# S5 powers, table and C moved to VectorE and ScalarE, and the first S5 chunk run through the K tiles together with one output-gate chunk

## The chip, the cores and the metric

The kernel runs on one core of one Trainium2 chip. The metric is the device time of one execution in microseconds (us); lower is better. The core's engines run side by side: TensorE (PE in the profile) multiplies matrices, and its weight loads (PEld) are listed apart; VectorE (DVE) and GpSimd (POOL) do element-wise work, ScalarE (ACT) does activations and copies, SyncE (SP) issues most transfers. Each engine carries out its own instructions in a fixed order.

## The reference

One layer of a streaming encoder over 272 positions (16 learned meta tokens and 256 inputs), width 2048, all in float32:

```
proj = rmsnorm(h) @ w_in                  # 2048 x 5120, columns q | f | i | g | u, 1024 each
o_hg = hgrn2(q, f, i) * norm * silu(g)    # gated linear recurrence, 8 heads of 128
y    = scan(x_t = A x_(t-1) + B u_t), C x # S5: 64 groups, 64 complex states each
o_s5 = rmsnorm(glu(gelu(y + d*u), w_glu)) # 1024 x 1024
h    = h + [o_hg, o_s5] @ w_out           # 2048 x 2048
h    = h + convffn(rmsnorm(h))            # w_gate, w_up, w_down with 5632 columns, width-3 convolution
out  = rmsnorm(h[16:])
```

S5 needs per state: the discretised A (`abr`, `xi`), its powers as cosines and sines of multiples of an angle, the factor (`zr`, `zi`) of B, and C.

## The kernel before, in words

**Weights.** Every weight matrix goes through in units of 1024 x 256 (1 MB): one DMA into a `raw` buffer (three of them), and then in two halves ACT rounds to `whi` and DVE takes the rest as `wlo` (L163 and L85, 128x1024 each; three buffers of each). A product is three matmuls, L187 (hi x hi), L188 (whi x low part of the input) and L189 (wlo x hi). The first two units (`early`) are split by DVE and POOL in quarters.

**Chunks.** A chunk of 256 columns of `w_in` is two units (K tiles 0 to 7 and 8 to 15) into two PSUM accumulators `acc` of 128 rows, 96 matmuls. There are 20 chunks: four each of u (S5), f, q, i (HGRN2; `do_h` runs one of each) and g (output gate). `ORDER` sets their order: u0 h0 u1 h1 u2 h2 u3 h3 g0 g1 g2 g3. The pool `pmm` has three accumulators; of the five other PSUM banks one, `psc`, serves the HGRN2 scores.

**Inputs.** xT is normalised K tile by K tile: `xn` on DVE, `xh` rounded on ACT, `xl` the rest on DVE (272 wide). The first chunk waits for these tiles one by one.

**S5 parameters.** About 60 instructions of 32 columns on DVE give `pw[0]` (cosine, sine of one step), abr, xi, zr, zi and the products zar, zai. POOL then makes eight more powers (`cpow`) and the table `ew` of 17 steps. C is loaded by SP, widened by two POOL copies, turned by 16 transposes, and DVE makes `cpc` from it in twelve instructions of 512 columns (two "kinds"). Scratch for this lies in two big tiles, `sca` and `scb`, which share their buffers (tags "gs" and "oT", one buffer each) with the tiles `gs` (gate times gain, all heads) and `oT` (HGRN2 output) that follow.

**Buffers.** A pool gives a buffer to the next tile of a tag only when every instruction that uses the earlier tile has run. In the pool `hgp` each tag has one buffer unless the line says otherwise; `sg` is the tag of the gate's sigmoid in `hg_g` and of q's in `hg_q`, and of `qt` in `hg_group`.

**Order on an engine.** The tool that builds the program orders each engine's instructions ahead of time: of those it takes for ready, the one of the highest priority. Priority is the order of the program text, shifted by `pri(...)`: weight splitting is moved up most (-4), reading accumulators by -3, `hg_group` by -2; the chunk's matmuls are moved down by 1.

The S5 scan of a group (`s5_scan`) and HGRN2's group work are mostly DVE work and run behind the chunks. After g3 the S5 part is finished: `gh` is made from the last S5 tile, then four w_glu chunks, then w_out.

Of the kernel before, what the change touches and what calls it, by code (L numbers as in the profile page):

```python
# [18 lines left out]
T = SEQ + NM  # L19
# [54 lines left out]
def hymba_kernel(ctx: ExitStack, tc: tile.TileContext, x, meta, lb_logits, norm_mix, w_in, hg_norm,  # L74
# [9 lines left out]
    def tt(dst, a, b, op, eng=dve):  # L84
        eng.tensor_tensor(out=dst, in0=a, in1=b, op=op)  # L85
# [82 lines left out]
    def colunit(w, k, c):  # L168
        return w[k * 1024:(k + 1) * 1024, c * 256:(c + 1) * 256].rearrange("(a p) n -> p a n", p=128)

    wpri = [1]

    def mm3(accs, units, rhs, n0, n1):

        last = len(units) - 1
        for ui, (u, k0) in enumerate(units):
            for hf, (hi, lo) in enumerate(u):
                for m in range(2):
                    for k in range(4):
# [39 lines left out]

    sca = ogp.tile([128, NH * NQ], F32, tag="gs", name="sca")  # L220
    scb = ogp.tile([128, NH * NQ], F32, tag="oT", name="scb")
    nrow = sca[0:KD, 256:384]

    xT = resp.tile([128, KD, T], F32, name="xT")
    hT = xT[:, :, T0:T]
# [1 line left out]
    sp.dma_start(out=ident, in_=c_ident)  # L227
    sp.dma_start(out=xm, in_=meta)
    HD = D // 2
    vrow = sca[0:100, 0:128]  # L230
    srow = sca[0:96, 128:256]
    lrow = prm.tile([96, 2], F32, name="lrow")
    crow = prm.tile([66, 2, 128], F32, name="crow")
    pool.dma_start(out=srow[0:32], in_=lam_re.rearrange("o (j g) p -> (o j) (g p)", g=2))
# [193 lines left out]
    tt(tz, zi, xi, MUL)
    tt(zar, zar, tz, SUB)
    tt(zai, zr, xi, MUL)  # L430
    tt(tz, zi, abr, MUL)
    tt(zai, zai, tz, ADD)
# [13 lines left out]
    tt(lbc[:, 0], le, le, SUB)  # L446
    ts(lbc[:, 1], lbc[:, 0], -1.0, MUL, 1.0, ADD)

    pt2 = prm.tile([128, 2, NP], F32, name="pt2")
    pt3 = prm.tile([128, 2, NP], F32, name="pt3")  # L450

    def cpow(dst, a, b):
        tt(pt2, pw[:, a, 1:3], pw[:, b, 1:2].to_broadcast([128, 2, NP]), MUL, pool)
        tt(pt3, pw[:, a, 0:2], pw[:, b, 2:3].to_broadcast([128, 2, NP]), MUL, pool)
        tt(pw[:, dst, 1:3], pt2, pt3, ADD, pool)
        ts(pw[:, dst, 0], pw[:, dst, 2], -1.0, MUL, 0.0, ADD, pool)

    for d_, a_, b_ in ((1, 0, 0), (2, 1, 1), (3, 2, 2), (4, 3, 3), (5, 4, 4), (6, 5, 1), (7, 6, 6), (8, 7, 7)):
        cpow(d_, a_, b_)
# [5 lines left out]
    et2 = scb[:, 1024:1536].rearrange("p (j s b) -> p j s b", j=NP, s=2)
    et3 = scb[:, 1536:2048].rearrange("p (j s b) -> p j s b", j=NP, s=2)
    for lv, n in ((1, 1), (2, 2), (3, 4), (4, 8)):
        cb = pw[:, lv, 1].unsqueeze(2).unsqueeze(3).to_broadcast([128, NP, 2, n])
        sb = pw[:, lv, 2].unsqueeze(2).unsqueeze(3).to_broadcast([128, NP, 2, n])
        tt(et2[:, :, :, 0:n], ew[:, :, 1:3, 0:n], cb, MUL, pool)  # L470
        tt(et3[:, :, :, 0:n], ew[:, :, 0:2, 0:n], sb, MUL, pool)
        tt(ew[:, :, 1:3, n:2 * n], et2[:, :, :, 0:n], et3[:, :, :, 0:n], ADD, pool)
        ts(ew[:, :, 0, n:2 * n], ew[:, :, 2, n:2 * n], -1.0, MUL, 0.0, ADD, pool)
    for k in range(3):
        dve.tensor_copy(out=ew[:, :, k, 16:17], in_=pw[:, 5, k].unsqueeze(2))


    cx = sca[:, 0:2048].rearrange("p (r b g q) -> p r b g q", r=2, b=8, g=2)
    craw = scb[:, 0:1024].rearrange("p (r b q) -> p r b q", r=2, b=8)
# [3 lines left out]
    cpc = s5p.tile([128, NP, 2, 2, S5H], F32, name="cpc")
    cq = [scb[:, 512 * i:512 * i + 512].rearrange("p (j h) -> p j h", h=S5H) for i in range(2)]
    ct = [sca[:, 512 * i:512 * i + 512].rearrange("p (j h) -> p j h", h=S5H) for i in range(2)]
    for ri in range(2):
        for hb in range(2):
            tp = ptp.tile([128, 4, 128], F32, tag="tp", name="ctp")
            with pri(LATE):
              for b in range(4):  # L490
                pe.transpose(tp[:, b], cx[:, ri, hb * 4 + b].rearrange("p a b -> p (a b)"), ident)
            for g in range(2):
                pr = slice(64 * g, 64 * g + 64)
                act.copy(out=cq[ri][pr, hb * 16:(hb + 1) * 16, :],
                         in_=tp[pr].rearrange("p b (j g h) -> p (b j) g h", g=2, h=S5H)[:, :, g])
    for kind, (wr, wi) in enumerate(((zr, zi), (zar, zai))):
        wrb = wr.unsqueeze(2).to_broadcast([128, NP, S5H])
        wib = wi.unsqueeze(2).to_broadcast([128, NP, S5H])
        tt(ct[0], cq[0], wrb, MUL)
        tt(ct[1], cq[1], wib, MUL)  # L500
        tt(cpc[:, :, kind, 0], ct[0], ct[1], SUB)
        tt(ct[0], cq[0], wib, MUL)
        tt(ct[1], cq[1], wrb, MUL)
        stt(cpc[:, :, kind, 1], ct[0], -1.0, ct[1], MUL, SUB)
# [67 lines left out]
    def s5_scan(P_, bu):  # L572

        W = s5w.tile([128, 3, TH], F32, tag="W", name="W", bufs=3)
        tmp = s5w.tile([128, 2, 68], F32, tag="tmp", name="tmp")
        act.copy(out=W[:, :, 0:17], in_=ew[:, P_])
        for lv, n in ((6, 17), (7, 34), (8, 68)):
            fact(tmp[:, :, 0:n], W[:, 0:2, 0:n], AF.Copy, scale=pw[:, lv, 2, P_:P_ + 1])
            stt(W[:, 1:3, n:2 * n], W[:, 1:3, 0:n], pw[:, lv, 1, P_:P_ + 1], tmp[:, :, 0:n], MUL, ADD)
# [197 lines left out]
        return accs  # L777


    def do_u(c):  # L780
        accs = chunk(w_in, 16 + c)
        with pri(-3):
            for m in range(2):
                s5_u(2 * c + m, accs[m])
        for m in range(2):
            s5_tile(2 * c + m, *s5_split(2 * c + m), *s5_b(2 * c + m))

    def do_h(g):
        accs = chunk(w_in, 4 + g)
# [270 lines left out]
```

## Time and profile before

| what | us |
|---|---|
| median of 3 runs (lowest, highest) | 1244.62 (1244.57, 1245.36) |
| the profiled execution's own time | 1245.69 |
| its span, first to last instruction | 1243.9 |
| PE busy in the span | 1219.3 |
| DVE busy | 881.3 |
| ACT busy | 601.2 |
| POOL busy | 116.9 |

Times in the trace count from the span's start. A matmul's record is longer than the distance to the next one, because matmuls are pipelined; the distance from start to start is its cost. DVE records overlap a little in the same way. "Idle before <- releaser" is how long the engine stood before an instruction, and what ended the wait.

### The profile page before, as it was taken

The numbers are of one execution on the slowest core, as the hardware profiler recorded it, in microseconds if no ns is written. First come the engines' busy times: TensorE is split into PE (matmuls) and PEld (weight loads), VectorE is DVE, ScalarE is ACT, GpSimd is POOL, SyncE is SP. The second block draws the span as 40 slices with busy tenths as digits, with TensorE's granted clock in tenths as the row PEclk, the third lists the DMA queues.
The fourth block names the chain that finished last, engine by engine and source line by source line (L and its number), as shares of the span: only waits on it lengthen the run. The fifth ranks groups of instructions, "written<-read, shape, count | busy, mean of one in ns | idle before, by whom it ended". The sixth has DMA issues, their size and how long they took to land.

```text
span 1243.9 us, 22660 instructions
## 1 busy us (share of the span) xinstructions
PE 1219.3 (98%) x9235; PEld 1144.6 (92%) x9235; DVE 881.3 (71%) x1504; ACT 601.2 (48%) x1046; POOL 116.9 (9%) x166
## 2 busy tenths in 40 slices
PE   7979999999999999999999999999999999999997
PEld 6979999989988999999999999999999988888886
DVE  8899999999968777765656656656656644555554
ACT  5646666665555455433433433434333434444454
POOL 5483132121100000000000000000000000000000
PEclk9989999999999999999999999999999999999999
DMA  8434444344335556555555655555565645555552
GB/s 255 143 125 123 130 126 127 110 140 137 129 115 164 170 176 198 169 192 182 182 192 173 198 172 193 180 183 191 174 199 170 228 162 189 200 199 183 193 206 99
DMA packets 176295, 210.73 MB, mean 169 GB/s; under 512 B 14772, under 2 KB 168879, under 8 KB 170415
## 3 DMA queue, kind: packets, MB, share of 16 engines
q1 hardware_dynamic: 175871, 209.20, 51.4%
q8 instruction: 72, 1.18, 0.4%
q14 instruction: 32, 0.26, 0.1%
q0 software_dynamic: 320, 0.09, 0.0%
HBM read 206.05 MB, written 2.10 MB: 167 GB/s over the span
## 4 chain that ended last, share of the span: by engine, by line
PE 94%; DVE 4%; DMA 0%; issue 0%; ACT 0%; SPq 0%; DVEq 0%; ACTq 0%
PE acc L189 9%; PE acc L187 9%; PE acc L188 9%; PE ua L188 7%; PE ua L187 7%; PE ga L187 7%; PE ua L189 7%; PE ga L189 7%; PE ga L188 7%; PE d L983 6%; PE d L981 6%; PE d L982 6%; PE bu L603 1%; PE lps L732 1%; DVE wlo L85 1%; DVE xn L94 1%
## 5 line engine op out<-in xcount | busy, mean ns | idle before, releaser
L85 DVE TENSOR_TENSOR wlo<-raw,whi 128x1024 fp32r<-128x1024 f32 (+1 forms) x376 | 461.0, 1226 | 309.3 <-ACT whi L163 259.8
L163 ACT CAST whi<-raw 128x1024 fp32r<-128x1024 f32 (+1 forms) x382 | 397.8, 1042 | 527.2 <-PE ga L188 158.2
L187 PE MATMUL ga<-fh,whi 128*128 128x258 f32 x704 | 199.0, 283 | 0.5 <-DVE a L85 0.5
L189 PE MATMUL ga<-fh,wlo 128*128 128x258 f32 x704 | 198.5, 282 | 0.0
L188 PE MATMUL ua<-fl,whi 128*128 128x256 f32 x704 | 198.4, 282 | 0.0
L188 PE MATMUL ga<-fl,whi 128*128 128x258 f32 x704 | 198.1, 281 | 0.0
L189 PE MATMUL ua<-fh,wlo 128*128 128x256 f32 x704 | 197.9, 281 | 0.0
L187 PE MATMUL ua<-fh,whi 128*128 128x256 f32 x704 | 197.9, 281 | 0.0
L189 PE MATMUL acc<-xh,wlo 128*128 128x272 f32 (+1 forms) x640 | 186.5, 295 | 7.1 <-DVE wlo L85 7.1
L188 PE MATMUL acc<-xl,whi 128*128 128x272 f32 (+1 forms) x640 | 186.0, 292 | 3.8 <-DVE xl L85 3.8
L187 PE MATMUL acc<-xh,whi 128*128 128x272 f32 (+1 forms) x640 | 186.5, 294 | 0.4 <-ACT PP L82 0.4
L187 PEld LDWEIGHTS ga<-fh,whi 128*128 128x128 f32 x704 | 133.0, 189 | 0.7 <-DVE a L85 0.7
L188 PEld LDWEIGHTS ga<-fl,whi 128*128 128x128 f32 x704 | 133.4, 190 | 0.0
L187 PEld LDWEIGHTS ua<-fh,whi 128*128 128x128 f32 x704 | 133.1, 189 | 0.0
L189 PEld LDWEIGHTS ua<-fh,wlo 128*128 128x128 f32 x704 | 132.9, 189 | 0.0
L188 PEld LDWEIGHTS ua<-fl,whi 128*128 128x128 f32 x704 | 132.8, 189 | 0.0
L189 PEld LDWEIGHTS ga<-fh,wlo 128*128 128x128 f32 x704 | 132.6, 188 | 0.0
L189 PEld LDWEIGHTS acc<-xh,wlo 128*128 128x128 f32 x640 | 121.5, 191 | 11.0 <-DVE wlo L85 7.7
L188 PEld LDWEIGHTS acc<-xl,whi 128*128 128x128 f32 x640 | 121.8, 190 | 7.0 <-DVE xl L85 4.8
L981 PE MATMUL d<-whi,ah 128*128 128x512 f32 x328 | 127.7, 389 | 0.0
L982 PE MATMUL d<-whi,al 128*128 128x512 f32 x328 | 127.6, 389 | 0.0
L187 PEld LDWEIGHTS acc<-xh,whi 128*128 128x128 f32 x640 | 121.6, 191 | 4.3 <-issue 1.9
(383 smaller groups left out, 1856.5 us busy)
## 6 DMA issues: line engine op xcount, KB each, us to landing
raw<-in_w_ffn_gate SPq DMA_DIRECT2D x44, 1024.0 KB, 5.1
raw<-in_w_ffn_up SPq DMA_DIRECT2D x44, 1024.0 KB, 5.1
raw<-in_w_ffn_down SPq DMA_DIRECT2D x44, 1024.0 KB, 4.8
raw<-in_w_in SPq DMA_DIRECT2D x39, 1024.0 KB, 5.1
raw<-in_w_out SPq DMA_DIRECT2D x16, 1024.0 KB, 5.3
raw<-in_w_glu SPq DMA_DIRECT2D x4, 1024.0 KB, 5.1
x<-in_x SPq DMA_DIRECT2D x4, 512.0 KB, 5.6
out<-ob SPq DMA_DIRECT2D x8, 256.0 KB, 2.7
```

The source lines that it names most:

```text
L85: eng.tensor_tensor(out=dst, in0=a, in1=b, op=op)
L94: dve.scalar_tensor_tensor(out=dst, in0=a, scalar=s, in1=b, op0=op0, op1=op1, **kw)
L163: act.copy(out=hi[:, c], in_=raw[:, hf, c])
L187: pe.matmul(accs[m], lh, xh[:, n0:n1], start=first, stop=False)
L188: pe.matmul(accs[m], lh, xl[:, n0:n1], start=False, stop=False)
L189: pe.matmul(accs[m], ll, xh[:, n0:n1], start=False, stop=end)
L603: return pe.matmul(bus[i][:, ri], bt[h, 2 * ri + q0 // 2], R[h, q0 // 2], start=True, stop=True)
L732: pe.matmul(ps[:, i], kt[:, i], qf[:, 64 * i:64 * (i + 1)], start=True, stop=True)
L981: pe.matmul(dps[t][n], ah[:, tk], hi, start=False, stop=False, skip_group_check=True)
L982: pe.matmul(dps[t][n], al[:, tk], hi, start=False, stop=False, skip_group_check=True)
L983: pe.matmul(dps[t][n], ah[:, tk], lo, start=False, stop=end, skip_group_check=True)
```

## The change

What it does, part by part:

- POOL's powers and table move to DVE. The angle doubling needs three small DVE instructions (`square`) instead of four on POOL; one of the eight powers is a general product. The sign row of `pw` is dropped. The table `ew` is made by twelve DVE instructions; its sign row comes from ACT.
- C: the two widening copies move from POOL to ACT; zar and zai are dropped; `c_kinds(hb)` makes both kinds for one half of the states, eight DVE instructions. The first half is made with the parameters, the second half in `do_u` after chunk u1. Both use the upper half of `sca` as scratch, the table the lower half. The rows of parameters that lay in sca lie in scb.
- `ORDER` becomes ug0 h0 u1 h1 u2 h2 u3 h3 g1 g2 g3. `do_ug(0)` runs u0 and g0 together: for each half unit first u0's 24 matmuls, then g0's 24. Four accumulators are used, three of pmm and the one of psc. The second early unit is g0's. After the chunk `hg_g` is called for heads 0 and 1, so `gs` gets its first columns here.

```diff
-ORDER = "u0 h0 u1 h1 u2 h2 u3 h3 g0 g1 g2 g3"
+ORDER = "ug0 h0 u1 h1 u2 h2 u3 h3 g1 g2 g3"
...
-    early.append(wload(colunit(w_in, 1, U0)))
+    early.append(wload(colunit(w_in, 0, 12)))
...
-    zar, zai = st("zar"), st("zai")
-    tt(zar, zr, abr, MUL)
...
-    def cpow(dst, a, b):
-        tt(pt2, pw[:, a, 1:3], pw[:, b, 1:2].to_broadcast([128, 2, NP]), MUL, pool)
...
+    def square(d_, a_):
+        stt(pt, pw[:, a_, 1], -2.0, pw[:, a_, 1], MUL, MUL)
+        stt(pw[:, d_, 1], pw[:, a_, 0], 2.0, pw[:, a_, 1], MUL, MUL)
+        ts(pw[:, d_, 0], pt, 1.0, ADD)
...
-        pool.tensor_copy(out=cx[:, ri], in_=craw[:, ri].unsqueeze(2).to_broadcast([128, 8, 2, S5P]))
+        act.copy(out=cx[ri], in_=craw[:, ri].unsqueeze(2).to_broadcast([128, 8, 2, S5P]))
...
+    et2, et3 = (sca[:, 512 * i:512 * i + 512].rearrange("p (j s b) -> p j s b", j=NP, s=2) for i in range(2))
+    for lv, n in ((1, 1), (2, 2), (3, 4), (4, 8)):
+        tt(et2[:, :, :, 0:n], ew[:, :, 1:3, 0:n], cb, MUL)
+        tt(et3[:, :, :, 0:n], ew[:, :, 0:2, 0:n], sb, MUL)
+        tt(ew[:, :, 1:3, n:2 * n], et2[:, :, :, 0:n], et3[:, :, :, 0:n], ADD)
+        fact(ew[:, :, 0, n:2 * n], ew[:, :, 2, n:2 * n], AF.Copy, scale=-1.0)
...
+    def c_kinds(hb):
+        hs_ = slice(16 * hb, 16 * hb + 16)
+        for d_, sv, (ar, ai) in ((0, ccx[:, hs_], (zr, zi)), (1, cpc[:, hs_, 0:1], (abr, xi))):
+            dv = cpc[:, hs_, d_:d_ + 1]
+            t_ = [sca[:, 1024 + 512 * i:1536 + 512 * i].rearrange("p (j k r h) -> p j k r h", k=1, r=2, h=S5H)
+                  for i in range(2)]
+            for z, w in zip(t_, (ar, ai)):
+                tt(z.rearrange("p j k r h -> p j (k r h)"), sv.rearrange("p j k r h -> p j (k r h)"),
+                   w[:, hs_].unsqueeze(2).to_broadcast([128, 16, 32]), MUL)
+            tt(dv[:, :, :, 0], t_[0][:, :, :, 0], t_[1][:, :, :, 1], ADD)
+            tt(dv[:, :, :, 1], t_[0][:, :, :, 1], t_[1][:, :, :, 0], SUB)
+
+    c_kinds(0)
...
+    def do_ug(c):
+        gacc = [pmm.tile([128, NQ], F32, tag="mm", name="acc"), psc.tile([128, NQ], F32, tag="sc", name="acc")]
+        accs = [pmm.tile([128, T], F32, tag="mm", name="acc") for _ in range(2)]
...
+            for hf in range(2):
+                mm3(accs, uu, xr, 0, T, part=(k, hf))
+                mm3(gacc, gu, xr, T0, T, part=(k, hf))
+        do_u(c, accs)
+        with pri(-3):
+            hg_g(2 * c, gacc)
...
+        if c == 1:
+            c_kinds(1)
```

## Rows read from the trace of the kernel before

**Rows 1.** The page: busy tenths of DVE in 40 slices of 31 us.

```profile
DVE  8899999999968777765656656656656644555554
```

**Rows 2.** Waits of PE over the span: total us, times, longest.

```profile
PE acc L189 <- DVE wlo L85: 7.3, 4, 6.4
PE acc L188 <- DVE xl L85: 3.8, 3, 1.7
...
PE acc L187 <- ACT PP L82: 0.4, 1, 0.4
```

**Rows 3.** Windows: PE, PEld, DVE, ACT, POOL busy us (count), granted clock, DMA.

```profile
30.00:32.00 2.00, 2.00 (x9) 2.00 (x10) 2.00 (x7) 1.72 (x4) 0.00 (x0) 0.50 1.08 380
...
84.00:86.00 2.00, 2.00 (x10) 2.00 (x10) 2.00 (x3) 0.39 (x1) 1.92 (x3) 0.50 1.02 349
```

**Rows 4.** Timeline of PE: start us, duration us; from the start of i through the long stall.

```profile
64.60 0.29 PE L187 MATMUL acc<-xh,whi 128*128 128x272 f32 x1
...
66.24 0.29 PE L188 MATMUL acc<-xl,whi 128*128 128x272 f32 x1
...
75.80 0.29 PE L188 MATMUL acc<-xl,whi 128*128 128x272 f32 x1
82.46 0.59 PE L189 MATMUL acc<-xh,wlo 128*128 128x272 f32 x1 [6.37 <-DVE wlo L85]
...
86.70 0.43 PE L188 MATMUL acc<-xl,whi 128*128 128x272 f32 x1
```

**Rows 5.** Timeline of DVE: normalisation, then the last C instruction.

```profile
16.60 1.74 DVE L94 SCALAR_TENSOR_TENSOR xn<-xT,gm,rbs 128x272 f32<-128x272 f32 x4
...
30.79 0.48 DVE L94 SCALAR_TENSOR_TENSOR xn<-xT,gm,rbs 128x272 f32<-128x272 f32 x1
31.20 0.43 DVE L85 TENSOR_TENSOR xl<-xn,xh 128x272 fp32r<-128x272 f32 x1
...
33.45 1.27 DVE L94 SCALAR_TENSOR_TENSOR xn<-xT,gm,rbs 128x272 f32<-128x272 f32 x1
...
39.69 1.19 DVE L94 SCALAR_TENSOR_TENSOR e1p<-e1p,e1r 128x32 f32<-128x32 f32 x5
...
86.01 0.81 DVE L94 SCALAR_TENSOR_TENSOR cpc<-sca 128x512 f32<-128x512 f32 x1
```

**Rows 6.** Timeline of POOL: a widening copy, the first and last power.

```profile
33.09 1.35 POOL L482 COPY sca<-scb 128x1024 f32<-128x1024 f32 x1 [3.80 <-PE sps L353]
...
88.15 0.27 POOL L91 TENSOR_SCALAR pw<-pw 128x32 f32<-128x32 f32 x1
```

**Rows 7.** DVE groups between 50 and 95 us: busy us, mean ns of one.

```profile
L85 DVE TENSOR_TENSOR wlo<-raw,whi 128x1024 fp32r<-128x1024 f32 x10 | 12.9, 1292 | 1.5 <-ACT whi L163 1.5
...
L85 DVE TENSOR_TENSOR sca<-scb,zai 128x512 f32<-128x512 f32 x2 | 2.0, 1014 | 0.0
...
L85 DVE TENSOR_TENSOR sca<-scb,zar 128x512 f32<-128x512 f32 x2 | 1.4, 684 | 0.0
```

**Rows 8.** DVE groups between 100 and 330 us, where POOL is mostly idle.

```profile
L85 DVE TENSOR_TENSOR wlo<-raw,whi 128x1024 fp32r<-128x1024 f32 x54 | 67.1, 1242 | 2.9 <-ACT whi L163 2.8
L589 DVE TENSOR_TENSOR_SCAN m<-r,m 128x136 f32<-128x136 f32 x58 | 22.6, 426 | 2.6 <-POOL m L85 2.6
L85 DVE TENSOR_TENSOR P<-W,m 128x544 f32<-128x544 f32 x30 | 21.4, 715 | 0.1
...
L85 DVE TENSOR_TENSOR kt<-k,SP 128x256 f32<-128x256 f32 x16 | 6.7, 420 | 0.0
```

**Rows 9.** Waits of DVE between 30 and 62 us.

```profile
DVE wlo L85 <- ACT whi L163: 2.6, 4, 1.5
```

**Rows 10.** Tiles gs and gh: duration min/median/max ns, first and last start us.

```profile
L94 DVE SCALAR_TENSOR_TENSOR gs<-acc,vcol,sg x8: 472/476/487, 314.4 to 366.6; 128x258 f32<-128x258 f32 x8
...
L187 PE MATMUL acc<-gh,whi x64: 276/281/291, 364.3 to 389.4; 128*128 128x258 f32 x64
...
L85 DVE TENSOR_TENSOR gh<-ysb,gh x8: 420/422/423, 355.2 to 357.5; 128x258 fp32r<-128x258 f32 x8
```

More of the change, by code (lines that the diff above doesn't have):

```diff
@@ L171, in hymba_kernel, with mm3 @@
     wpri = [1]
-    def mm3(accs, units, rhs, n0, n1):
+    def mm3(accs, units, rhs, n0, n1, part=None):
         last = len(units) - 1
-        for ui, (u, k0) in enumerate(units):
+        for ui, (u, k0) in enumerate(units) if part is None else ((part[0], units[part[0]]),):
             for hf, (hi, lo) in enumerate(u):
+                if part is not None and hf != part[1]:
+                    continue
                 for m in range(2):
@@ L221, in hymba_kernel @@
     scb = ogp.tile([128, NH * NQ], F32, tag="oT", name="scb")
-    nrow = sca[0:KD, 256:384]
+    nrow = scb[0:KD, 256:384]
     xT = resp.tile([128, KD, T], F32, name="xT")
@@ L229, in hymba_kernel @@
     HD = D // 2
-    vrow = sca[0:100, 0:128]
-    srow = sca[0:96, 128:256]
+    vrow = scb[0:100, 0:128]
+    srow = scb[0:96, 128:256]
     lrow = prm.tile([96, 2], F32, name="lrow")
@@ L392, in hymba_kernel @@
     fact(sh, ph, AF.Sin, scale=0.5)
-    NPW = [1, 2, 4, 8, 16, 32, 34, 68, 136]
-    pw = s5p.tile([128, len(NPW), 3, NP], F32, name="pw")
+    pw = s5p.tile([128, 9, 2, NP], F32, name="pw")
     c1, md = st("c1"), st("md")
@@ L402, in hymba_kernel @@
     ts(md, md, -0.5, MUL, 1.5, ADD)
-    tt(pw[:, 0, 1], c1, md, MUL)
-    tt(pw[:, 0, 2], s1, md, MUL)
-    ts(pw[:, 0, 0], pw[:, 0, 2], -1.0, MUL)
+    tt(pw[:, 0, 0], c1, md, MUL)
+    tt(pw[:, 0, 1], s1, md, MUL)
     xr, den, zr, zi, tz = st("xr"), st("den"), st("zr"), st("zi"), st("tz")
     abr, xi = st("abr", s5p), st("xi", s5p)
-    tt(abr, rr, pw[:, 0, 1], MUL)
+    tt(abr, rr, pw[:, 0, 0], MUL)
     ts(xr, abr, -1.0, ADD)
-    tt(xi, rr, pw[:, 0, 2], MUL)
+    tt(xi, rr, pw[:, 0, 1], MUL)
     r2 = st("r2", s5p)
@@ L425, in hymba_kernel @@
     tt(zi, zi, den, MUL)
-    zar, zai = st("zar"), st("zai")
-    tt(zar, zr, abr, MUL)
[L428 to L432, printed above, removed]
     lz = st("lz", tag="s1")[:, 0:NH]
@@ L447, in hymba_kernel @@
     ts(lbc[:, 1], lbc[:, 0], -1.0, MUL, 1.0, ADD)
-    pt2 = prm.tile([128, 2, NP], F32, name="pt2")
-    pt3 = prm.tile([128, 2, NP], F32, name="pt3")
-    def cpow(dst, a, b):
-        tt(pt2, pw[:, a, 1:3], pw[:, b, 1:2].to_broadcast([128, 2, NP]), MUL, pool)
[L454 to L459, printed above, removed]
+    pt = st("pt", tag="s1")
+    def square(d_, a_):
+        stt(pt, pw[:, a_, 1], -2.0, pw[:, a_, 1], MUL, MUL)
+        stt(pw[:, d_, 1], pw[:, a_, 0], 2.0, pw[:, a_, 1], MUL, MUL)
+        ts(pw[:, d_, 0], pt, 1.0, ADD)
+    for a_ in range(5):
+        square(a_ + 1, a_)
+    p2 = [prm.tile([128, 2, NP], F32, name=f"p2{i}") for i in range(2)]
+    for i in range(2):
+        tt(p2[i], pw[:, 5], pw[:, 1, i:i + 1].to_broadcast([128, 2, NP]), MUL)
+    tt(pw[:, 6, 0], p2[0][:, 0], p2[1][:, 1], SUB)
+    tt(pw[:, 6, 1], p2[0][:, 1], p2[1][:, 0], ADD)
+    square(7, 6)
+    square(8, 7)
     ew = s5p.tile([128, NP, 3, 17], F32, name="ew")
@@ L464, in hymba_kernel @@
     dve.memset(ew[:, :, 2, 0:1], 0.0)
[L465 to L479, printed above, removed]
+    craw = sca[:, 0:1024].rearrange("p (r b q) -> p r b q", r=2, b=8)
+    cx = [z[:, 1024:2048].rearrange("p (b g q) -> p b g q", b=8, g=2) for z in (scb, sca)]
+    cpc = s5p.tile([128, NP, 2, 2, S5H], F32, name="cpc")
+    ccx = s5p.tile([128, NP, 1, 2, S5H], F32, name="ccx")
     for ri, c in enumerate((c_re, c_im)):
         sp.dma_start(out=craw[:, ri], in_=c.rearrange("o (b g) h p -> (o g h) b p", b=8))
-        pool.tensor_copy(out=cx[:, ri], in_=craw[:, ri].unsqueeze(2).to_broadcast([128, 8, 2, S5P]))
[L483 to L487, printed above, removed]
+        act.copy(out=cx[ri], in_=craw[:, ri].unsqueeze(2).to_broadcast([128, 8, 2, S5P]))
+    for hb in range(2):
+        for ri in range(2):
             tp = ptp.tile([128, 4, 128], F32, tag="tp", name="ctp")
@@ L490, in hymba_kernel @@
               for b in range(4):
-                pe.transpose(tp[:, b], cx[:, ri, hb * 4 + b].rearrange("p a b -> p (a b)"), ident)
+                pe.transpose(tp[:, b], cx[ri][:, hb * 4 + b].rearrange("p a b -> p (a b)"), ident)
             for g in range(2):
                 pr = slice(64 * g, 64 * g + 64)
[L494 to L504, printed above, removed]
+                fact(ccx[pr, hb * 16:(hb + 1) * 16, 0, ri, :],
+                     tp[pr].rearrange("p b (j g h) -> p (b j) g h", g=2, h=S5H)[:, :, g], AF.Copy,
+                     scale=(1.0, -1.0)[ri])
@@ new lines, in hymba_kernel @@
+    et2, et3 = (sca[:, 512 * i:512 * i + 512].rearrange("p (j s b) -> p j s b", j=NP, s=2) for i in range(2))
+    for lv, n in ((1, 1), (2, 2), (3, 4), (4, 8)):
+        cb = pw[:, lv, 0].unsqueeze(2).unsqueeze(3).to_broadcast([128, NP, 2, n])
+        sb = pw[:, lv, 1].unsqueeze(2).unsqueeze(3).to_broadcast([128, NP, 2, n])
+        tt(et2[:, :, :, 0:n], ew[:, :, 1:3, 0:n], cb, MUL)
+        tt(et3[:, :, :, 0:n], ew[:, :, 0:2, 0:n], sb, MUL)
+        tt(ew[:, :, 1:3, n:2 * n], et2[:, :, :, 0:n], et3[:, :, :, 0:n], ADD)
+        fact(ew[:, :, 0, n:2 * n], ew[:, :, 2, n:2 * n], AF.Copy, scale=-1.0)
@@ new lines, in hymba_kernel @@
+    act.copy(out=ew[:, :, 1:3, 16:17].rearrange("p j s b -> p s (j b)"), in_=pw[:, 5])
+    fact(ew[:, :, 0, 16:17].rearrange("p j b -> p (j b)"), pw[:, 5, 1], AF.Copy, scale=-1.0)
+    def c_kinds(hb):
[9 more added lines that the diff above has]
+            tt(dv[:, :, :, 1], t_[0][:, :, :, 1], t_[1][:, :, :, 0], SUB)
@@ L577, in s5_scan @@
         for lv, n in ((6, 17), (7, 34), (8, 68)):
-            fact(tmp[:, :, 0:n], W[:, 0:2, 0:n], AF.Copy, scale=pw[:, lv, 2, P_:P_ + 1])
-            stt(W[:, 1:3, n:2 * n], W[:, 1:3, 0:n], pw[:, lv, 1, P_:P_ + 1], tmp[:, :, 0:n], MUL, ADD)
+            fact(tmp[:, :, 0:n], W[:, 0:2, 0:n], AF.Copy, scale=pw[:, lv, 1, P_:P_ + 1])
+            stt(W[:, 1:3, n:2 * n], W[:, 1:3, 0:n], pw[:, lv, 0, P_:P_ + 1], tmp[:, :, 0:n], MUL, ADD)
             fact(W[:, 0, n:2 * n], W[:, 2, n:2 * n], AF.Copy, scale=-1.0)
@@ L777, in chunk, with do_u @@
         return accs
-    def do_u(c):
-        accs = chunk(w_in, 16 + c)
+    def do_ug(c):
+        gacc = [pmm.tile([128, NQ], F32, tag="mm", name="acc"), psc.tile([128, NQ], F32, tag="sc", name="acc")]
+        accs = [pmm.tile([128, T], F32, tag="mm", name="acc") for _ in range(2)]
+        xr = lambda kt: (xh[:, kt], xl[:, kt])
+        uu, gu = [None, None], [None, None]
+        for k in range(2):
+            uu[k] = (wunit(colunit(w_in, k, 16 + c)), k * 8)
+            gu[k] = (wunit(colunit(w_in, k, 12 + c)), k * 8)
+            for hf in range(2):
[4 more added lines that the diff above has]
+            hg_g(2 * c, gacc)
+    def do_u(c, accs=None):
+        accs = accs or chunk(w_in, 16 + c)
         with pri(-3):
@@ L809, in hymba_kernel @@
     for o in ORDER.split():
-        {"u": do_u, "h": do_h, "g": do_g}[o[0]](int(o[1]))
+        {"u": do_u, "h": do_h, "g": do_g, "ug": do_ug}[o.rstrip("0123456789")](int(o[-1]))
     s5ws.close()
```

## The prediction

> **What bounds the kernel now.** The page comes first: PE is busy for 1219.3 of 1243.9 us, so the change can win back at most the 24.6 us in which PE stands, and what it loses to a low clock. The view of waits says where they are: 3.8 us for xl, 7.3 for wlo, the longest 6.4 [rows 2]. Both lie before 90 us. The windows show that each is followed by a stretch at a granted clock of 0.50, that is 1.2 instead of 2.4 GHz [rows 3]. The timeline of PE prices this: at full clock 13 steps of the i chunk take 66.24 - 64.60 us, 0.126 each, so a chunk of 96 takes 12.1 us (11.5 for the 258-wide ones); after the long stall, 19 matmuls fill 82.46 to 86.70, 0.23 each, about 2.0 us lost [rows 4]. So the first stall costs 3.8 + 1.1 us (nine slow matmuls in the window [rows 3], two beside it), the second 6.4 + 2.0, with 0.7 of shorter waits ahead of it: 14.0 us.
>
> Behind the second stall stands DVE. Its busy slices are full up to some 340 us [rows 1]; 6.4 us long PE had nothing to multiply because a wlo stood in DVE's line behind HGRN2 and C work. In the first 90 us the kernel is bound by DVE, and after that by PE, with DVE's backlog hidden under it. The question is therefore what DVE must finish before PE may go on, in the old and in the new order.
>
> **What the change does to DVE, part by part.** DVE works from 16.60 on [rows 5]. Its records overlap: xn 0.41 us from start to start against a duration of 0.48, so about 0.07 comes off each duration.
>
> *C.* The old twelve instructions lie in six groups of two with means from 0.68 to 1.01 us [rows 7], 10.0 us together, 9.2 without the overlap. The new ones: for each half and kind two of 512 columns at 0.62 (0.684 - 0.07) and two of 256 at 0.35 (0.42 - 0.07) [rows 7, 8], 1.94; four times that is 7.8. zar and zai (six instructions of 32 columns, 1.3 us) go.
>
> *Powers.* 25 small instructions. Where one waits for the one ahead it costs 0.24 (five in 1.19 us [rows 5]), where others fill in, about 0.11: from 2.8 to 6.0 us. I take 3.4, since weight splits and other chains are there to fill in.
>
> *Table.* Twelve instructions of 64, 128, 256 and 512 columns, three each: estimates of 0.18, 0.25, 0.35 and 0.62 between the small row and the 512 row, 4.2 us. The sign rows on ACT cost PE nothing: ACT is busy 48% of the span; without that cover they would add four waits of some 0.5 us.
>
> *POOL's silence.* POOL runs powers up to 88.15 [rows 6]. Under its copy of 1.35 us at 33.09, an xn takes 1.27 instead of 0.48 [rows 5, 6]; a wlo between 50 and 95 takes 1.292 on average, 1.242 later [rows 7, 8]. Two copies give 1.6 us; wlo, small instructions and HGRN2's between 52 and 87 give 2.9: 4.5 us that DVE gets back, beside C's own. The Trainium skill (SBUF — State Buffer, Who interferes with whom) says that a DVE instruction with two SBUF inputs and a POOL instruction that reads SBUF shut each other out, the loser for the whole instruction. The xn row agrees, the wlo mean does not look like a loss of whole instructions; by that rule alone POOL could have cost DVE many times the 4.5 us, and I go by the rows.
>
> *The joint chunk.* u0 and g0 need two units each through DVE; the early ones are split mostly by POOL, so DVE sees one half unit more than before up to the same point: +1.1 us. On PE it fills the wait for xl: g0's matmuls use the K tiles that are there. That is worth up to 4.9 us, if nothing later takes it back. The transfers are the same ones in another order, and SP's queue passes nothing that is needed earlier.
>
> **The wait that the change adds.** `hg_g` now writes gs at the joint chunk. Before, gs was first written at 314.4 us [rows 10] and sca, whose buffer it takes, was last used at 86.01 [rows 5]. Now sca's last user is `c_kinds(1)`, which lies behind chunk u1 in the program. The first gs therefore waits for the parameters, the table and both halves of C, whatever columns they use. What waits behind it: g0's two accumulators (one of pmm's three and psc), and the one `sg` buffer. f still gets two accumulators. q gets them too, but its sigmoid needs `sg`, so q stays in PSUM, and the i chunk has no accumulator. PE then stands until gs is written.
>
> *When q ends.* The chunks start some 2 us behind the first xn, near 18.7. 12.1 + 11.5 for the joint chunk, estimates of 1.0 for waits and 2.2 for transposes between its matmuls, then f 12.1 and q 11.5, with 0.4 between chunks as in [rows 2]: about 70 us.
>
> *When gs is written.* From 16.60 to the end of the last C instruction at 86.8 [rows 5] are 70.2 us; DVE waited 2.9 of them, mostly for whi [rows 9]: 67.3 us of work. Of this, 2.8 no longer comes ahead (q, qt, qh, one SP, the copies into ew). 67.3 - 9.2 - 1.3 - 2.8 - 4.5 + 1.1 + 3.4 + 4.2 + 7.8 = 66.0. The whi waits stay (3.0), since they come from slots that PE frees. S5 scans stand ahead of `c_kinds(1)` in priority; a group costs DVE about 2.8 us (two P at 0.65, two scans at 0.36, xo and three W [rows 8]); bounds are none and four groups, 11 us, and I take one: the chain of a scan goes through ACT and POOL and leaves gaps for C. With the gs instruction itself (0.48): 16.6 + 66.0 + 3.0 + 2.8 + 0.5 = 88.9, say 89 us. PE stands for some 19 us, from 70 to 89.
>
> **The sum.** i then takes 12.1 + 2.0 (low clock again), and u1 starts at 103.1. Before, about 17 matmuls of i were left at 82.46 and u1 started near 86.3, with 0.3 of slow matmuls to come. g0's 11.5 us are already done: 103.1 - 86.3 - 0.3 - 11.5 = +5.0 us. From there on PE has the same work. S5's tail does not bind: it has the same DVE work by the clock, and PE comes later. On the profiled execution's 1245.7 that makes 1250.7; the median of the runs is 1.1 lower: 1249.6.
>
> The bounds: with powers at 2.8, no scan ahead and the whi waits filled, gs is written near 82 (-2 us); with four groups of scans or powers at 6.0, near 97 to 100 (+13 to +16).
>
> A rule of the Trainium skill speaks to the same place: Perfetto Trace Analysis (Optimization Strategy) says that a recurring gap on the engine that should be full can mean that the next tile finds no buffer. The trace of before has one wait for an accumulator, 0.4 us for the reading of f [rows 2], so by that row alone the joint chunk would be free.
>
> **The rivals.**
>
> *The hold does not bind* (gs is written before q ends). For it: the first stall shows that PE runs ahead of DVE, and C by halves is less DVE work. Against it: 14 us or more of DVE work would have to vanish before 70. Then 14.0 us of stalls are open to gain, but w_glu's first matmul, at 364.3 before, cannot come before gh: its first DVE part came at 355.2 [rows 10], so at most some 8.5 us of it stay unless DVE ends its tail earlier: 1244.6 - 8.5 = 1236.1. It decides once gs is written by 76 or so; by 84 the result is zero.
>
> *POOL's silence is worth more.* If POOL holds up some twelve more DVE instructions by the 0.8 us of the xn row, DVE gets back 10 us more than the 4.5, gs is written at 79 and the time falls by 5: 1239.6. Against it: the wlo mean [rows 7, 8]. The rule of the Trainium skill's page SBUF — State Buffer (Who interferes with whom) would make this the likelier case; here the mean over ten wlo decides.
>
> *The scans go first.* If four groups stand ahead, the stall grows by 8 us more: 1258.
>
> **How the numbers follow.** About 0.2% (2.5 us) is what a measurement of this kernel can tell from no change. My forecast, with gs written between 86.5 and 93, I give 0.42 (1247 to 1254); scans first 0.13; both are slower: 0.55. gs between 82 and 86.5 gives no change: 0.20. POOL's silence 0.10 and no hold 0.15 are faster: 0.25. The range from 1237 to 1258 leaves out most of the no-hold case and the far end of the scans, 0.2 together.
>
> **What would show it.** Right: a single PE wait of 15 us or more between 65 and 95 us, at the first matmul of i, released by the reading of an accumulator; the first gs just behind the last C instruction on DVE; no xl wait over 1 us; glu later than 364 by 5. Wrong: gs written before 70 with PE running on; or C's second half ahead of the table's end; powers above 6 us; a wait of PE at gh near 355, which would mean that the gain was made early and given back at the tail.

## The result, and the profile after

The changed kernel takes 1257.6 us (median of 4 runs, 1256.53 to 1258.83) against 1244.59 (1244.38 to 1245.36): a ratio of 1.0098, interval 1.0086 to 1.011, some 13 us slower. The profiled execution took 1258.83 us with a span of 1257.0, where before it was 1245.69 and 1243.9. The sign is the predicted one and the time lies inside the range, but the loss is 13 us and not 5.

The waits of PE, which answer to [rows 2], show one predicted stall and one that nobody predicted:

```profile
PE acc L189 <- DVE gs L94: 10.3, 1, 10.3
PE bps L886 <- DVE hr L85: 3.4, 1, 3.4
PE acc L191 <- DVE wlo L85: 3.1, 2, 2.9
...
PE acc L190 <- DVE xl L85: 0.6, 1, 0.6
```

The first is the hold. The timeline of DVE (start, duration) answers to the end of [rows 5]: the second half of C is done at 76.4, the last level of the table at 84.9, and then the first two gs follow. Between C and the table lies, among others, a reciprocal of 3.34 us.

```profile
75.73 0.75 DVE L85 TENSOR_TENSOR cpc<-sca 128x256 f32<-128x256 f32 x2
...
76.96 3.34 DVE L706 RECIPROCAL rv<-SP 128x512 f32<-128x512 f32 x1
...
82.23 1.47 DVE L85 TENSOR_TENSOR sca<-ew,pw 128x512 f32<-128x512 f32 x2
...
84.16 0.77 DVE L85 TENSOR_TENSOR ew<-sca 128x512 f32<-128x512 f32 x1
84.86 0.62 DVE L85 TENSOR_TENSOR p<-pw 128x64 f32<-128x64 f32 x2
85.40 0.87 DVE L94 SCALAR_TENSOR_TENSOR gs<-acc,vcol,sg 128x258 f32<-128x258 f32 x2
```

On PE, the same stretch (beside [rows 4]): the first matmul of the i chunk waits for that gs, and the 23 matmuls up to 91.31 go by at 0.23 us each, at a granted clock of 0.50 (1.2 of 2.4 GHz) in the window of 85 to 90.

```profile
75.23 0.36 PE L554 MATMUL ktp<-cp,eb 128*32 128x32 f32 x16 [1.23 <-ACT bt L550]
85.93 0.59 PE L189 MATMUL acc<-xh,whi 128*128 128x272 f32 x1 [10.34 <-DVE gs L94]
...
91.31 0.29 PE L191 MATMUL acc<-xh,wlo 128*128 128x272 f32 x1
```

The second stall lies 300 us later, where HGRN2's half of w_out begins. These are windows (columns as in [rows 3]); the kernel before has 30 to 44 matmuls in each of them at a granted clock of 1.00.

```profile
390.00:395.00 5.00, 1.95 (x4) 1.06 (x4) 3.78 (x9) 2.42 (x6) 0.00 (x0) 0.67 0.64 211
395.00:400.00 5.00, 5.00 (x20) 4.30 (x20) 4.42 (x13) 0.82 (x2) 0.00 (x0) 0.50 0.01 2
400.00:405.00 5.00, 5.00 (x27) 4.04 (x26) 3.51 (x10) 1.87 (x3) 0.00 (x0) 0.81 0.00 0
405.00:410.00 5.00, 2.07 (x12) 1.61 (x11) 5.00 (x12) 3.62 (x10) 0.00 (x0) 0.87 0.00 0
410.00:415.00 5.00, 4.83 (x20) 4.08 (x20) 3.76 (x11) 0.81 (x2) 0.00 (x0) 0.50 0.66 210
```

What is late there is `hr`, the reciprocal root of HGRN2's last norm, which every row of HGRN2's half of mh needs. The timeline of PE shows its first user, then the next head's, and w_out's first matmuls between them at half speed:

```profile
389.38 0.28 PE L191 MATMUL acc<-gh,wlo 128*128 128x258 f32 x1
393.05 0.58 PE L886 MATMUL bps<-hr,hsel 40*128 40x258 f32 x1 [3.40 <-DVE hr L85]
...
394.72 0.58 PE L886 MATMUL bps<-hr,hsel 40*128 40x258 f32 x1
395.23 1.01 PE L189 MATMUL acc<-mh,whi 128*128 128x258 f32 x3
...
397.46 0.58 PE L886 MATMUL bps<-hr,hsel 40*128 40x258 f32 x1
...
409.34 0.58 PE L191 MATMUL acc<-mh,wlo 128*128 128x258 f32 x1 [2.93 <-DVE wlo L85]
```

A head's bps must be followed by two DVE instructions and one of ACT before its rows of mh and ml can be multiplied, so PE goes head by head, up to 401.7 at half speed. At 406.4 it stops again for 2.9 us, for a wlo that stands on DVE behind eight instructions of S5's norm, and up to 415.4 it is once more at half speed. The two waits are 6.3 us; the two stretches at half speed cost some 6 us, an estimate from 45 matmuls of w_out at 0.21 us from start to start instead of 0.12, and seven small ones. Together that is nearly the whole loss.

hr hangs on a chain that can't start before h3's i chunk is read (iv). The tiles iv, gs, gh and hr say where the change puts them; the last two numbers of the times are the first and the last start. Of the kernel before:

```profile
L662 ACT COPY iv<-acc x8: 359/380/388, 85.1 to 300.4; 128x272 f32<-128x272 f32 x8
...
L856 PE MATMUL hps<-sq,misc x16: 381/381/386, 355.3 to 366.1; 128*8 128x258 f32 x16
...
L85 DVE TENSOR_TENSOR hr<-rhy,hr x1: 419/419/419, 379.6 to 379.6; 8x258 fp32r<-8x258 f32 x1
```

Of the changed kernel (gs and gh answer to [rows 10]):

```profile
L663 ACT COPY iv<-acc x8: 372/384/388, 102.5 to 316.2; 128x272 f32<-128x272 f32 x8
...
L94 DVE SCALAR_TENSOR_TENSOR gs<-acc,vcol,sg x8: 473/478/480, 85.4 to 360.4; 128x258 f32<-128x258 f32 x8
...
L189 PE MATMUL acc<-gh,whi x64: 277/284/388, 358.1 to 389.1; 128*128 128x258 f32 x64
...
L85 DVE TENSOR_TENSOR gh<-ysb,gh x8: 419/420/422, 340.3 to 343.0; 128x258 fp32r<-128x258 f32 x8
...
L85 DVE TENSOR_TENSOR hr<-rhy,hr x1: 418/418/418, 392.6 to 392.6; 8x258 fp32r<-8x258 f32 x1
```

S5's tail (gh) is 15 us earlier than before, and w_glu begins at 358.1 instead of 364.3. Yet h3's i is read 15.8 us later, hr is ready at 393.0 instead of 380.1, 12.9 us later, and the end comes 13.1 us later. Where w_glu begins, the change looks like a gain of 6 us. Where it ends, the two kernels are level: its last hi x hi matmul starts at 389.1, and at 389.4 before [rows 10]. Part of the 6 us was work that had only moved: the matmuls of hps lay mostly ahead of w_glu before (355.3 to 366.1) and lie within it now (369.5 to 378.7). So the whole loss appears behind w_glu, in w_out.

### The profile page after: what moved, and what is told of

The parts are those of the page before. It is cut to its first block, busy times and chain, and to the rows that moved or that the text cites. A ratio compares the mean times of both kernels' runs of the same rounds, so it can differ in the third digit from the quotient of the medians.

```text
span 1257.0 us, 22646 instructions
## 1 busy us (share of the span) xinstructions
PE 1223.2 (97%) x9235; PEld 1147.9 (91%) x9235; DVE 878.8 (70%) x1535; ACT 610.0 (49%) x1055; POOL 88.1 (7%) x116
## 4 chain that ended last, share of the span: by engine, by line
PE 92%; DVE 5%; ACT 1%; DMA 1%; issue 0%; POOL 0%; SPq 0%; DVEq 0%; ACTq 0%
PE acc L189 9%; PE acc L190 9%; PE acc L191 9%; PE ua L190 7%; PE ua L189 7%; PE ga L189 7%; PE ua L191 7%; PE ga L191 7%; PE ga L190 7%; PE d L1001 6%; PE d L1000 6%; PE d L1002 6%; PE bu L604 1%; PE lps L733 1%; DVE wlo L85 1%; DVE xn L94 1%
## 5 line engine op out<-in xcount | busy, mean ns | idle before, releaser
L189 PE MATMUL acc<-xh,whi 128*128 128x272 f32 (+1 forms) x640 | 185.9, 294 | 10.3 <-DVE gs L94 10.3
L189 PEld LDWEIGHTS acc<-xh,whi 128*128 128x128 f32 x640 | 121.2, 190 | 12.3 <-DVE gs L94 10.4
```

## The experiments

Two theories stood at the start. *The hold* (B): the stall at 75 to 86 us costs its own length and the low clock behind it. *The cover* (A, later D): HGRN2's last chain, from h3's i to hr, sets the end, because only three g chunks stand behind it instead of four; the hold matters through what it makes late. All runs, with what the traces say of the chain ("i of h3": start of its last reading; hr: when it is ready, its start plus 0.42 us). The last five columns are in us and come from the one execution that was profiled, which need not be the median one:

| run | us, median | ratio to before (interval) | first i | i of h3 | hr | span | span - hr |
|---|---|---|---|---|---|---|---|
| before | | | 85.1 | 300.4 | 380.1 | 1243.9 | 863.8 |
| changed | 1257.6 | 1.0098 (1.0086, 1.011) | 102.5 | 316.2 | 393.0 | 1257.0 | 864.0 |
| e1_scratch | 1237.0 | 0.9935 (0.992, 0.995) | 87.9 | 303.5 | 365.8 | 1236.2 | 870.4 |
| e2_h3first | 1254.09 | 1.0074 (1.0059, 1.0089) | 102.1 | 299.8 | 373.5 | 1254.1 | 880.6 |
| e3_s5only | 1242.72 | 0.9986 (0.9973, 1.0) | 81.6 | 293.4 | 370.2 | 1243.7 | 873.5 |
| e4_joint | 1263.84 | 1.0145 (1.0128, 1.0162) | 107.9 | 325.6 | 398.8 | 1264.1 | 865.3 |
| e5_g1early | 1251.96 | 1.0052 (1.0037, 1.0067) | 88.3 | 317.7 | 386.9 | 1249.6 | 862.7 |
| e6_delay | 1251.08 | 1.0046 (1.0029, 1.0063) | 99.6 | 311.3 | 386.3 | 1249.0 | 862.7 |
| e7_normup | 1257.79 | 1.0096 (1.0081, 1.0111) | 100.0 | 313.8 | 390.6 | 1254.2 | 863.6 |
| e8_h3low | 1237.86 | 0.9939 (0.9924, 0.9954) | 88.2 | 301.2 | 367.4 | 1235.4 | 868.0 |
| e9_onestep | 1252.45 | 1.0053 (1.0038, 1.0068) | 100.7 | 314.5 | 384.7 | 1248.6 | 863.9 |
| e10_u3early | 1256.41 | 1.0088 (1.0073, 1.0103) | 88.0 | 310.7 | 391.5 | 1254.5 | 863.0 |
| e11_jointfree | 1247.4 | 1.0016 (1.0006, 1.0025) | 103.8 | 317.0 | 384.7 | 1245.2 | 860.5 |
| e12_before1 | 1245.6 | 0.9997 (0.9987, 1.0007) | 87.1 | 302.4 | 376.6 | 1245.0 | 868.4 |

**Another scratch (e1_scratch).** The scratch of `c_kinds` and of the table moves to scb; sca is then free after the C transposes.

```diff
-    et2, et3 = (sca[:, 512 * i:512 * i + 512]...
+    et2, et3 = (scb[:, 1024 + 512 * i:1536 + 512 * i]...
-            t_ = [sca[:, 1024 + 512 * i:1536 + 512 * i]...
+            t_ = [scb[:, 512 * i:512 * i + 512]...
```

> The changed kernel with another scratch: the products of C lie in the lower half of scb, the table's in its upper half; sca is then last read by the C transposes (58.3 us in the changed kernel), and the first gs no longer waits for table and C. Theory A (cover): the 13 us are lost behind h3, where three g chunks instead of four cover HGRN2's last chain. DVE is full up to some 340 us, so the chain from h3's i to hr ends little earlier; the wait of 10.3 us at i goes, and most of it comes back as waits at w_glu or w_out: 1250 to 1257 us. Theory B (hold): the wait of 10.3 us and the low clock behind it, some 12 us together, are the loss: 1244 to 1247 us.

Measured 1237.0 us, below both ranges. The first gs is written at 59.2, and PE waits for no accumulator any more:

```profile
PE acc L189 <- ACT gh L845: 2.0, 1, 2.0
PE acc L191 <- DVE wlo L85: 1.9, 1, 1.9
```

So without the hold the kernel is 20.6 us faster, twice the wait of 10.3. Theory A as first stated (VectorE gives nothing back) is wrong; theory B names the right culprit and half of its price. hr is ready 27 us earlier though first i and h3's i come only 14.6 and 12.7 us earlier: the chain between them has become 14.5 us shorter too. What ends this kernel's stage is gh: the wait of 2.0 us at 357.2, the first w_glu matmul.

**h3 ahead of u3 (e2_h3first).** The changed kernel with `... u2 h2 h3 u3 g1 g2 g3`.

> The changed kernel with h3 ahead of u3 in ORDER, all else the same, the hold too. Theory A (cover): h3's i is read about 12 us earlier (near 302 instead of 314 to 316), hr is ready near 381, no wait for hr or wlo over 1 us at w_out and no granted clock of 0.50 there: 1243 to 1247 us. Theory B (hold): no difference, 1256 to 1259 us. A third way: the last S5 tile is now late, a wait of 5 us or more at gh ahead of w_glu takes what the cover gives: 1250 to 1262 us.

Measured 1254.09: theory A's 1243 to 1247 missed. h3's i and hr do come 16.4 and 19.5 us earlier, but now the last S5 tile is late; w_glu begins at 374.6 instead of 358.1. The time is that of the third way, its sign is not: PE stands 3.8 us for hr, whose first user lies ahead of w_glu here, and then only 0.6 for gh. Both tails, S5's to gh and HGRN2's to hr, end within 1.1 us of each other; they share the same cover.

**The two halves of the change (e3_s5only, e4_joint, e11_jointfree).** e3 has the new S5 code with the old ORDER and early units. e4 has the new ORDER, `do_ug` and mm3's `part`, with the old S5 code. e11 is e4 with the products of C in tiles of their own:

```diff
-    ct = [sca[:, 512 * i:512 * i + 512].rearrange("p (j h) -> p j h", h=S5H) for i in range(2)]
+    ct = [prm.tile([128, NP, S5H], F32, name=f"ct{i}") for i in range(2)]
```

> Only the S5 part of the change (powers and table on VectorE, C by halves, copies on ACT), with the order and the early units of the kernel before: no joint chunk, gs first written behind h3. Theory A: four g chunks cover h3's chain again and nothing is held; the first wait for xl (3.8 us) stays, the second (6.4 us for wlo and 2 us of low clock) shrinks: 1237 to 1244 us. Theory C (the work moved to VectorE is what costs): the wait for wlo near 76 us stays or grows, 1245 to 1252 us.

> Only the joint chunk and the new order, with the S5 code of the kernel before (powers and table on POOL, C in one piece with its products in sca). Theory A: both losses are there, a wait at i until the last C instruction (near 87 us, so 12 us or more) and the stall at w_out: 1257 to 1266 us. Theory B (hold alone): 1250 to 1258 us, with no wait over 1 us at w_out. Theory C (the work moved to VectorE costs): 1240 to 1248 us.

> Joint chunk and new order with the S5 code of the kernel before, as in the run with 1263.8 us, but with the products of C in two tiles of their own, so that sca is last read by the C transposes and the first gs is not held. If the hold is what that run lost: 1240 to 1246 us, and the joint chunk alone is worth 0 to 5 us. If powers and table on POOL (to 88 us in the kernel before) are the point, the first S5 groups wait for them and PE with them: 1248 to 1262 us.

The S5 part alone gives 1242.72, in the expected range and 2.9 us under the kernel before, with an interval that reaches to no difference (its ten runs go from 1241.91 to 1248.55, and the profiled one took 1245.49); PE's waits for wlo fall from 7.3 to 4.0. The joint chunk alone gives 1263.84, in the range of "both losses". With the hold taken away it gives 1247.4, between the two ranges: 16.4 us come back, but nothing is won over the kernel before. The waits of its DVE (60 to 92 us) and of its PE say why:

```profile
DVE ew L477 <- POOL pw L85: 6.4, 1, 6.4
```

```profile
PE acc L191 <- DVE wlo L85: 12.3, 1, 12.3
```

DVE stands for a power of POOL, and the next wlo comes only 6.4 us later in its order, behind C and the reciprocal. So e11 has no hold (its first gs starts at 60.5) but a stall of the same length: in e4, too, PE stands 12.3 us, there for S5's part of C, with gs at 85.6 right behind. What e11 wins back it therefore wins later, with hr 14.2 us earlier; this pair does not show what the hold alone costs. By the medians, the two halves need each other: on the old S5 code the joint chunk is worth nothing, on the new one 5.7 us (1242.72 to 1237.0).

**Less cover without a hold (e5_g1early), delay without a hold (e6_delay).** Both start from e1. e5 has `u3 g1 h3 g2 g3`; e6 puts 98 matmuls ahead of h0's i chunk.

```diff
+        for _ in range(extra):
+            with pri(wpri[0]):
+                pe.matmul(accs[0], xh[:, 0, 0:128], xh[:, 1], start=True, stop=True)
```

> The kernel with the other scratch (no hold, 1237.0 us), with g1 ahead of h3 in ORDER: two g chunks instead of three behind h3. Theory D (the last chain): from the reading of h3's i to hr it took 61.8 us with the other scratch, 76.4 in the changed kernel and 79.2 in the kernel before; h3's i is now read near 315 us, about where it was in the changed kernel (316.2), hr is ready between 377 and 392, PE stands or runs at a clock of 0.50 at w_out as in the changed kernel: 1243 to 1256 us. Theory B (the hold is all of it): nothing is held, so 1235 to 1239 us.

> The kernel with the other scratch (no hold, 1237.0 us), with 98 matmuls more (128x272, 0.126 us each, 12.3 us) ahead of h0's i chunk, whose product is overwritten: PE is late by as much as the hold made it, at the same place, but no buffer is held and PE does not stand. Theory D: h3's i is read near 316 us, the last chain is late by as much, and w_out waits for it as in the changed kernel: 1250 to 1258 us. Theory B (the wait costs its own length): 1249 to 1250 us. Theory E (VectorE sets the end of the stage and PE has room): 1237 to 1243 us.

e5: 1251.96, as theory D expects and far from B's 1235 to 1239. Nothing is held, h3's i is read at 317.7, and w_out stalls as in the changed kernel. e6: 1251.08. The time lies in D's range, but only 1 us above B's, so the trace must decide: the extra 12.3 us put first i 11.7 us later, w_glu only 2.9 us later (360.1 against 357.2), and hr 20.5 us. Up to w_glu the delay is nearly absorbed; at w_out it is back, as in these windows of e6:

```profile
390.00:395.00 5.00, 3.66 (x15) 2.81 (x16) 3.83 (x10) 1.90 (x6) 0.00 (x0) 0.79 0.59 190
395.00:400.00 5.00, 5.00 (x30) 4.41 (x30) 2.94 (x9) 1.66 (x3) 0.00 (x0) 0.87 0.01 2
```

So a delay of PE costs at this place even where no buffer is held: 14.1 us by the medians, for 12.3 us of matmuls. Of the 20.5 us at hr, 7.8 are there at h3's i, and by 12.7 the chain behind it is longer. The rest of the 20.6 us that the hold costs, some 6 us, is not explained by the delay alone and stays open.

**Shortening the chain itself (e7_normup, e9_onestep, e12_before1).** e7 raises the last norm block of the changed kernel; e9 and e12 take two of three steps out of its root, in the changed kernel and in the kernel before.

```diff
-    with pri(-2):
+    with pri(-4.5):
         hps = psc.tile([8, NQ], F32, tag="sc", name="hps")
```

```diff
-        for _ in range(3):
+        for _ in range(steps):
...
-        hrs = rsqrt(hgp, hps, [8, NQ], 1.0 / 128, "rh", tags=("iv", "qm", "v"))
+        hrs = rsqrt(hgp, hps, [8, NQ], 1.0 / 128, "rh", tags=("iv", "qm", "v"), steps=1)
```

> The changed kernel, hold and all, with HGRN2's last block (hps to ml) raised from -2 to -4.5, above the weight splits. Theory D: from hps to hr on VectorE takes 13.5 us in the changed kernel, with a wlo in between six times; without them hr is ready 5 to 8 us earlier, the wait for hr (3.4 us) and the low clock after it go: 1246 to 1253 us. Rival: the weight splits that are now behind become late, 1255 to 1262 us; or the block is paced by ACT and PE and nothing moves, 1256 to 1259 us.

> The changed kernel, hold and all, with one step instead of three in the reciprocal root of HGRN2's last norm (hrs is then less exact): six small instructions less between hps and hr, nothing less on PE. In six runs so far (before, changed, joint chunk alone, g1 early, 98 matmuls more, norm raised) the span ended 863 to 865 us behind the moment in which hr was ready. Theory D (hr sets the end): hr is ready 6 to 9 us earlier than 393.0, and the time falls by nearly as much, 1249 to 1253 us. Theory B (the hold's own length): 1256 to 1259 us.

> The kernel before with the same single step in HGRN2's last norm (hrs less exact). hr was ready there at 380.1 us, and w_out started at 389.8 at three quarters of the usual rate (30 to 34 matmuls in 5 us against 43). If hr sets the end there too: 1238 to 1241 us. If four g chunks cover the chain in full: 1243 to 1246 us, no difference.

e7 moved nothing: from the reading of hps (376.8) to hr ready (390.6) it still takes 13.8 us (13.9 in the changed kernel, where four wlo lie in between and not the six of the expectation). The four are still there in e7, in the same places, so the edit did not shorten the chain and says nothing on what a shorter one would give. e9 is the clean test: six small DVE instructions less, hr ready at 384.7 instead of 393.0 (1.7 us of these 8.3 are there already at h3's i, which the edit doesn't touch), and the span is 8.4 us shorter. By the medians it is 5.2 us: the changed kernel's profiled execution is its slowest of four, that of e9 its fastest. With the same edit the kernel before does not move (0.9997): there four g chunks cover the chain, though barely, since its hr stands no further ahead of the end than in the changed kernel.

The last column of the table says the same. In the nine executions with hr ready at 380 or later, the span ends 860.5 to 865.3 us behind hr, though hr itself moves by 18.7 us. In the other five (e1, e2, e3, e8, e12) that distance is larger, and there the end keeps another one: 878.5 to 880.8 us behind the first matmul of w_glu, which starts at 357.2, 374.6, 362.9, 356.9 and 366.2. Among the nine only the kernel before has this distance too (364.3, so 879.6); in the others it is 887 us and more. So the end follows the later of two things, w_glu's start and hr, and in the kernel before both came due together. This is read from fourteen traces; no run was made for it.

**Two tries at a faster one (e8_h3low, e10_u3early).** Both from e1: h3's group work at its own rank (`pri(0 if g == 3 else -2)`), and `u2 u3 h2 h3`.

> The kernel with the other scratch (no hold, 1237.0 us), with the group work of h3 alone at its place in the program instead of -2, so that the last S5 tile goes ahead of it on VectorE. With the other scratch hr was ready at 365.7 us, long before w_out, while w_glu waited 2.0 us for gh and ran at clocks of 0.83 for 10 us. Theory D: gh comes earlier and the spare time of hr pays for it: 1231 to 1235 us. If the chain from h3's i then becomes as long as in the changed kernel (76 us from 303.5, hr at 380) the time stays under 1237 still. Rival: hr becomes the late one, 1238 to 1245 us.

> The kernel with the other scratch (1237.0 us), with u3 ahead of h2 in ORDER. There gh was late (wait of 2.0 us at w_glu) and hr had some 20 us to spare. Theory D: S5's last tile is done earlier, PE reaches w_glu 3 to 8 us earlier, h3's i is read at about the same time as before (303.5), hr near 366 to 378 still before w_out: 1229 to 1235 us. Rival: HGRN2's chain of h3 is pushed back by the S5 work and hr becomes the late one: 1238 to 1248 us.

e8: 1237.86, no difference to e1 beyond the intervals; w_glu still begins at 356.9, so the rank of h3's work is not what makes gh late. e10: 1256.41, above both ranges, by the rival's mechanism: h3's i is read at 310.7, hr is ready at 391.5, and the end lies 863.0 behind it. e1 stays the fastest kernel by the medians, 8.6 us under the one before; e8 can't be told from it.

## Why the prediction was wrong

*What bounds the first 90 us* was right, and so were the terms of DVE's work. C: the sixteen instructions add up to 7.8 us from start to start, most of them 0.60 for 512 columns and 0.34 for 256 (predicted 7.8). These groups of DVE between 16 and 90 us (busy, mean ns) give the powers and the table:

```profile
L94 DVE SCALAR_TENSOR_TENSOR pt<-pw 128x32 f32<-128x32 f32 x7 | 1.4, 199 | 0.0
...
L89 DVE TENSOR_SCALAR pw<-pt 128x32 f32<-128x32 f32 x7 | 1.3, 181 | 0.0
L94 DVE SCALAR_TENSOR_TENSOR pw<-pw 128x32 f32<-128x32 f32 x7 | 1.3, 180 | 0.0
...
L85 DVE TENSOR_TENSOR sca<-ew,pw 128x512 f32<-128x512 f32 x2 | 1.5, 776 | 0.0
...
L85 DVE TENSOR_TENSOR ew<-sca 128x512 f32<-128x512 f32 x1 | 0.8, 774 | 0.0
```

And between 50 and 95 us, as in [rows 7]:

```profile
L85 DVE TENSOR_TENSOR wlo<-raw,whi 128x1024 fp32r<-128x1024 f32 x8 | 9.7, 1213 | 0.9 <-ACT whi L163 0.9
```

With the general product's four instructions (1.0) and 0.07 us of overlap off each of 25, the powers are 3.2 us (predicted 3.4); all twelve of the table 5.4 less 0.8, 4.5 (4.2). POOL, busy for 36.6 of the 45 us between 50 and 95 before and for 13.1 now, shows in wlo: 1.213 us on average against 1.292 [rows 7]. The Trainium skill (SBUF — State Buffer, Who interferes with whom) would have let DVE lose whole instructions to POOL; a mean that falls by 6% bears out the rows.

*The hold* was right in place and cause. The first gs started at 85.4 and PE went on at 85.93, where 89 was predicted: no scan went ahead. The last to leave sca was the table and not `c_kinds(1)`. q's last matmuls were issued at 73.3, not 70, so the stall was 10.3 us (11.6 with the short wait ahead of it), not 19. The sum at this place still held: first i is read 17.4 us later than before, less the 11.5 of g0 that are done, +5.9 against the predicted +5.0. That is in part luck: PE went on 3 us early, but the i chunk took some 17 us and not 14.1, because 24 small matmuls of HGRN2 and S5 (dps, lps, bu) lie among its own. At h3's i it is 15.8 - 11.5 = +4.3, and at the end of w_glu nothing is left of it. The Trainium skill (Perfetto Trace Analysis, Optimization Strategy) says of a gap that repeats that it can mean a missing buffer. Here a single gap, of 10.3 us, had that cause: it went when the scratch moved to another buffer.

*The step that failed* is "From there on PE has the same work", and with it the check behind it: "S5's tail does not bind". S5's tail did not bind. The other tail did. The sum gave the change credit for g0's 11.5 us, as if PE's line were all that counts. But g0 had been cover: in the kernel before it stood behind h3 and kept PE busy while the chain from h3's i went through DVE, ACT and small matmuls to hr, 79.7 us later. That chain starts 15.8 us later by the clock and takes 76.8 us now: 15.8 - 2.9 = +12.9 at hr, +13.1 at the end. The credit is worth nothing here: 12.9 us of delay at hr came out as 13.1 at the end, so the cover in the kernel before had nothing left over (that it was enough, e12 shows). The prediction read gh, but never asked which chunk starts the chain to hr and how long it is; the rows were there (iv 300.4, hr 379.6, w_out's first matmul 389.8).

*The rivals.* "The hold does not bind" gave 1236.1, and e1, the kernel without it, took 1237.0, for the reason given there: w_glu can't begin before gh, whose first DVE part came at 357.2 where the prediction had read 355.2. "The scans go first" was wrong: no scan stands ahead of gs. Of the signs named beforehand, the xl wait is under 1 us as forecast (0.6), the stall is shorter than the 15 us named, and w_glu is 6 us early instead of 5 late. Of the signs of being wrong, one came true: C's second half was done before the table's end (76.4 and 84.9).

*What was luck.* With gs at 85.4 the prediction's own list gives "no change" (82 to 86.5 us). That the kernel is slower all the same, and that 1257.6 lies inside the range, comes from the tail that the prediction left out, and is no credit to its sum.

## What to carry to other kernels

Work that is moved to the front of the busy engine's line is a gain only if nothing behind its old place lived on it: for every chain that feeds a later stage, compare the time from the chunk that starts it to the chunk that needs it, before and after, by the clock and not by the work done. A tile that hands its buffer on waits for the last user in time, not for the one nearest in the text; here changed scratch offsets are worth 20.6 us. A stall early in a kernel can come back 300 us later, and the wait list then shows it under another name: taking away this one, of 10.3 us, gave twice its length, and a delay of 12.3 us without a hold cost 14.1.

## What the runs showed that was not expected

The same chain from h3's i to hr takes 62 to 81 us. One part of it depends on where its small matmuls fall in PE's fixed order. In the changed kernel the 16 hps matmuls lie among those of w_glu and take from 369.5 to 378.7; in e1, where they come ahead of w_glu's first matmul, from 351.3 to 354.8:

```profile
L875 PE MATMUL hps<-sq,misc x16: 381/381/385, 369.5 to 378.7; 128*8 128x258 f32 x16
```

```profile
L875 PE MATMUL hps<-sq,misc x16: 380/381/382, 351.3 to 354.8; 128*8 128x258 f32 x16
```

From the reading of hps to hr ready it is then 10.2 instead of 13.9 us, with one wlo in between on DVE instead of four. Of the 14.5 us between the two kernels these two parts make up some 9; the other 5.5 lie between h3's i and the first hps matmul (53.3 and 47.8 us). The longest chain, that of e10, is long only there (62.1 us), and why was not tested.
